# Turning the softmax weights, q and k of a layer on VectorE and GpSimd in place of TensorE and a round trip through DRAM

## The chip, the cores and the metric

The kernel runs on one core of one Trainium2 chip. A core has five engines that run side by side, each working through its own queue in order: TensorE (PE in the profile; its weight loads are PEld), VectorE (DVE), ScalarE (ACT), GpSimd (POOL) and SyncE (SP), which issues most DMAs. The metric is the device time of one execution in microseconds, as the median of several runs.

## What is computed

A two-layer encoder over 256 tokens of width 2048, batch 1, all in float32. Each layer has a mixer and a feed-forward part, both behind an RMS norm that is modulated by vectors made from a condition `c`. Cut to the part that the change touches:

```
h = rmsnorm(x) * (1 + scale) + shift
qa, ka, va, qb, kb, vb, ga, gb = split(h @ w_in)
qa, ka = rotary(rmsnorm(qa)), rotary(rmsnorm(ka))     # 8 query heads, 2 key heads of 128
qb, kb = rmsnorm(qb), rmsnorm(kb)                     # 8 heads of 128
ya = window_attention(qa, ka, va, sink) @ w_proj_a    # softmax(q k^T + mask) v, with a sink logit
yb = neighbourhood_attention(qb, kb, vb, bias) @ w_proj_b
x  = x + gate * ((sigmoid(ga) * ya + sigmoid(gb) * yb) @ w_out)
x  = x + gate2 * ((silu(conv(h2 @ w_up)_g) * conv(...)_v) @ w_down)
```

Two transposes hide in it. The projection gives q and k with tokens on the 128 partitions, and q k^T needs them with the head's 128 features there. The softmax gives its weights with queries on the partitions, and the product with v needs keys there.

## The kernel before

**The stream.** Each layer's weight matrices are cut into blocks of 128x128 in the order in which they are used, and 16 blocks make a unit of 1 MB, loaded by one DMA from SyncE's queue. A unit is used in two halves (`unit_steps`). Each float32 number is kept as a rounded high part and a remainder, so that three fast matmuls stand for one exact one: ScalarE casts a half to its high part (`hl`, L336) and VectorE subtracts to get the remainder (L337). Four half buffers turn round. TensorE consumes the stream in `features` (L355 to L357, output with features on the partitions, 256 columns) and in `tokens` (L418 to L420, tokens on the partitions, 512 columns); the nine column groups of q, k and v go through `tokens`, one group every four units.

**The background.** After each unit `Stream.tick` runs `bg.tick`: first what was put off to the next tick (`bg.defer`, `later`), then each background job by its pace, `ATT[l]` steps a tick for the attention while the q, k, v groups and the first gate pass, `ATT_B[l]` after the first projection. Other work is spread in between by plan, above all the modulation vectors: VectorE's multiply-and-reduce `aw` (L232). The order in which the instructions end up on each engine is made by a scheduler from the order of the program.

**q and k.** `qk_rows` takes a group's sums of squares on ScalarE (L588), a power -1/2 on GpSimd (`qrs`, L482), three ticks later the norm on VectorE (`qn`, L597) and, for the window heads, the rotary products and their sum and difference (L612 to L614). One tick later `turn` has TensorE transpose each head and half of the tokens into PSUM (`qtp`, L621), and ScalarE writes it with the gain into the group's `pack` (L622).

**A head.** `head_a` and `head_b` are generators that call `attend`; each `yield` is a step of the job, and in each step a new head starts and those under way advance. Scores on TensorE (`sc`, L648), maximum on VectorE (L651), exponential and division on ScalarE (L659, L667). Then, for heads that are not moved, four TensorE transposes (`tp`, L689); ScalarE and VectorE split the result into high part and remainder (`pT`, L430 and L431); a step later TensorE makes the output (`po`, L697). `MOVED[l]` gives how many window and neighbourhood heads of layer l are turned in another way: none but the eight neighbourhood heads of the second layer. For these VectorE transposes within blocks of 32x32 (L313), GpSimd's queue stores the rows block by block to DRAM (`pY`, L316, eight stores a head), and SyncE loads them back some ticks later (L299, two a head), the load held behind a subtraction of the stream (`BEHIND`).

Of the kernel before, what the change touches and what calls it, by code (L numbers as in the profile page):

```python
# [9 lines left out]
F32 = mybir.dt.float32  # L10
F32R = mybir.dt.float32r
AF = mybir.ActivationFunctionType
ALU = mybir.AluOpType
# [13 lines left out]
EPS = 1e-6  # L27
NEG = -1e30
SCALE = HEAD ** -0.5
BEHIND = mybir.DependencyInfo(mybir.DependencyClass.Sync, mybir.DependencyReason.DATA)  # L30
GRID_W, NA_KH, NA_KW = 64, 8, 16
BLOCK = 32

# [58 lines left out]
ADA_ORDER = [i for part in ADA_ORDER for i in part]  # L92
# [47 lines left out]
def encoder(ctx: ExitStack, tc: tile.TileContext, a: dict, out: bass.AP):  # L140
# [19 lines left out]
    dram = pool("dram", 2, space=bass.MemoryType.DRAM)  # L160

    ident = const.tile([P, P], F32, name="ident")
    make_identity(nc, ident[:])
# [43 lines left out]
    def paired(dt, name):  # L207

        t = ev.tile([P, 2 * S + ROW], dt, name=name, tag="u", bufs=2)
        return t[:, ROW - OFF : ROW - OFF + 2 * S].rearrange("p (a s) -> p a s", a=2)  # L210
# [71 lines left out]
                pass  # L282

    bg = Paced()
    halved = [None]

    def once(fn):

        due = [fn]

        def run():
            if due:
                due.pop()()

        return run

    def read_back(dst, src):

        tc.add_manual_dep(nc.sync.dma_start(dst, src).ins, halved[0], BEHIND)  # L299

    def later(n, fn):

        if n == 0:
            fn()
        else:
            bg.defer(lambda: later(n - 1, fn))

    def turned_blocks(p, rows, n, tag):

        y = dram.tile([P, n, S], F32, name=tag, tag=tag)  # L310
        to = y[:].rearrange("(b i) n (t a j) -> t a i n b j", i=BLOCK, t=2, a=P // BLOCK)
        for t, row in enumerate(rows):
            nc.vector.transpose(out=row, in_=p[t])  # L313
            src = row.rearrange("p (n b j) -> p n b j", n=n, j=BLOCK)
            for a in range(P // BLOCK):
                nc.gpsimd.dma_start(to[t, a], src[a * BLOCK : (a + 1) * BLOCK])  # L316
        return y

    def unit_steps(l, u, by_halves=False):

        raw = rawp.tile([P, UB * P], F32, name=f"w{l}_{u}", tag="raw")
        if not by_halves:
            nc.sync.dma_start(raw[:], a["ws"][l, u])
        halves = []
        streamed = any(m == "w_in" and mo < GATE_A // P for m, _, mo in STREAMS[l][u * UB : (u + 1) * UB])
        at = OFF if streamed else 0
        for j in range(2):
            n = UB * P // 2  # L330
# [5 lines left out]
            nc.scalar.copy(hl[:, 0], r)  # L336
            halved[0] = nc.vector.tensor_tensor(  # L337
                out=hl[:, 1], in0=r, in1=hl[:, 0].bitcast(F32), op=ALU.subtract
            ).ins.name
            halves.append(hl)  # L340
            if j == 0:
                yield halves
# [237 lines left out]
    def qk_rows(pss, heads, rot, gain, dst, then):  # L580
# [12 lines left out]
        rsqrt(rs[:, : 2 * heads], ss[:, : 2 * heads], HEAD, 2 * heads)  # L593
        def norm():
            qn = at.tile([P, 2, 4, HEAD], F32, name="qn", tag="qn", bufs=1)
            for t, ps in enumerate(pss):
                nc.vector.tensor_tensor(  # L597
                    out=qn[:, t, :heads],
                    in0=ps[:, cols : cols + n].rearrange("p (h d) -> p h d", d=HEAD),
                    in1=rs[:, t * heads : (t + 1) * heads].unsqueeze(2).broadcast_to([P, heads, HEAD]),  # L600
                    op=ALU.mult,
                )
            if rot is not None:
                x1, x2 = qn[:, :, :heads, :HALF], qn[:, :, :heads, HALF:ROT]
# [12 lines left out]
        def turn(qn):  # L617
            for t in range(2):
                ps = ax.tile([P, 4, P], F32, name="qtp", tag="ax")
                for h in range(heads):  # L620
                    nc.tensor.transpose(ps[:, h], qn[:, t, h], ident[:])  # L621
                nc.scalar.activation(  # L622
                    out=dst[:, :, t * P : (t + 1) * P], in_=ps[:, :heads], func=AF.Identity, scale=gain
                )
            then()

        bg.defer(lambda: bg.defer(lambda: bg.defer(norm)))
# [15 lines left out]
    def attend(q, k, v, p, mask, scale, sink, o, rows=None):  # L643
# [23 lines left out]
            nc.scalar.activation(out=p[:, t], in_=p[:, t], func=AF.Copy, scale=ri[:, t : t + 1])  # L667
        yield
        if rows is not None:
            rows = rows()  # L670
            y = turned_blocks([p[:, t] for t in range(2)], rows, 2, "pY")

            def back():
                for k in range(2):
                    read_back(rows[k], y[:, k])

            back = once(back)
            later(BACK[sink is None], back)
            yield
            yield  # L680
            back()
            pT = at.tile([P, 2, 2, S], F32R, name="pT", tag="pT", bufs=1)
            for k in range(2):
                split(pT[:, :, k], rows[k])
        else:
            tp = ax.tile([P, 2, S], F32, name="tp", tag="ax")
            for k in range(2):
                for t in range(2):
                    nc.tensor.transpose(tp[:, k, t * P : (t + 1) * P], p[:, t, k * P : (k + 1) * P], ident[:])  # L689
# [126 lines left out]
    for l in range(L):  # L816
# [41 lines left out]
        def head_a(i):  # L858
# [16 lines left out]
                return kvs[1]  # L875

            def rows():
                spare = ev.tile([P, S], F32, name=f"spare{l}_{i}", tag="r", bufs=2)
                return [qTa[:, i], spare[:]]
# [5 lines left out]
        def head_b(hb):  # L885
            b, i = packs[1 + hb // 4], hb % 4
            v = b[:, 4:8].rearrange("p (t a) s -> p t (a s)", t=2)
            p = at.tile([P, 2, S], F32, name="p", tag="p")
            nc.sync.dma_start(p[:], a["bias"][l, hb])
            q = in_halves(b[:, 8 + i], f"qB{l}_{hb}", "qh", l in SCORES_3)  # L890
            k = in_halves(b[:, i], f"kB{l}_{hb}", "kh", l in SCORES_3)
            yield
            yield from attend(
                q, k, lambda: in_halves(v[:, :, i * HEAD : (i + 1) * HEAD], f"vB{l}_{hb}", "vh", True), p, p, 1.0, None,
                lambda: oB_of(hb), (lambda: [b[:, 8 + i], b[:, i]]) if hb < MOVED[l][1] else None,
            )

        def oB_of(hb):
# [36 lines left out]
        for pi, (groups, gates) in enumerate(parts):  # L935
            last = pi == len(parts) - 1
            for g, part in enumerate(groups):
# [21 lines left out]
                    for t in range(2):  # L959
                        nc.scalar.copy(rows[:, t, vcol:], pss[t][:, vcol:])  # L960
                if g == 0:
                    qk_rows(pss, GA, rots[1], gains[:, 1:2], kTa, turned)
                elif g < 3:
                    qk_rows(pss, 4, rots[0], gains[:, 0:1], dst, turned)
                elif vcol is None:
                    qk_rows(pss, 4, None, gains[:, 3:4] if g in (3, 6) else gains[:, 2:3], dst, turned)
                else:
                    turned()
                if g == 2:
# [243 lines left out]
```

## Time and profile before

| | |
|---|---|
| Median of 3 runs | 2661.03 us (2660.66 to 2664.07) |
| Profiled execution, its own time | 2661.44 us |
| Its span in the trace | 2659.3 us |
| TensorE clock granted | full |
| Busy | PE 2647.6, PEld 2562.6, DVE 2106.2, ACT 1411.5, POOL 75.0 us |
| The second layer's q, k, v groups and heads | about 1400 to 1760 us |

Busy time is the time in which an engine had an instruction under way; an operation's row gives engine, line, output and inputs, shapes, count, then its busy time in us, the mean ns of one, and the idle time before it with what ended it. In a timeline the first two numbers are start and duration in us. The ends of matmuls are modelled, so matmuls are read by the distance of their starts. Times inside a part are from the start of the span.

### The profile page before, as it was taken

The numbers are of one execution on the slowest core, as the hardware profiler recorded it, in microseconds if no ns is written. First come the engines' busy times: TensorE is split into PE (matmuls) and PEld (weight loads), VectorE is DVE, ScalarE is ACT, GpSimd is POOL, SyncE is SP. The second block draws the span as 40 slices with busy tenths as digits, with TensorE's granted clock in tenths as the row PEclk, the third lists the DMA queues.
The fourth block names the chain that finished last, engine by engine and source line by source line (L and its number), as shares of the span: only waits on it lengthen the run. The fifth ranks groups of instructions, "written<-read, shape, count | busy, mean of one in ns | idle before, by whom it ended". The sixth has DMA issues, their size and how long they took to land.

```text
span 2659.3 us, 50973 instructions
## 1 busy us (share of the span) xinstructions
PE 2647.6 (100%) x21224; PEld 2562.6 (96%) x21224; DVE 2106.2 (79%) x2983; ACT 1411.5 (53%) x2292; POOL 75.0 (3%) x89
## 2 busy tenths in 40 slices
PE   9999999999999999999999999999999999999999
PEld 7888899999999999999998889999999999999999
DVE  8898998997987888788876666868888866655664
ACT  5445865456653554355554566555565445544553
POOL 0001100000000000000000001310000000000000
PEclk9999999999999999999999999999999999999999
DMA  9987789885777778788756666877747765555554
GB/s 365 349 327 297 264 300 351 321 311 212 290 295 286 296 290 287 288 297 296 295 205 256 236 229 238 299 264 261 278 179 287 297 251 191 191 197 194 196 191 143
DMA packets 106394, 704.63 MB, mean 265 GB/s; under 512 B 14001, under 2 KB 18353, under 8 KB 22321
## 3 DMA queue, kind: packets, MB, share of 16 engines
q1 hardware_dynamic: 104114, 699.27, 71.6%
q8 instruction: 166, 2.72, 0.4%
q0 software_dynamic: 2048, 2.10, 0.3%
q14 instruction: 66, 0.54, 0.1%
HBM read 697.13 MB, written 4.19 MB: 264 GB/s over the span
## 4 chain that ended last, share of the span: by engine, by line
PE 90%; DVE 5%; DMA 2%; ACT 1%; issue 1%; POOL 0%; DVEq 0%; ACTq 0%
PE ps L355 25%; PE ps L357 25%; PE ps L356 25%; PE ps_t L420 4%; PE ps_t L418 4%; PE ps_t L419 4%; DVE hl L337 2%; DVE aw L232 1%; DMA aw<-in_aw 1%; PE sc L648 1%; PE po L697 1%; ACT hl L336 1%; PE tp L689 0%; PE qtp L621 0%; DMA w<-in_ws 0%
## 5 line engine op out<-in xcount | busy, mean ns | idle before, releaser
L337 DVE TENSOR_TENSOR hl<-w,hl 128x1024 fp32r<-128x1024 f32 x928 | 1128.4, 1222 | 338.7 <-ACT hl L336 332.1
L336 ACT CAST hl<-w 128x1024 fp32r<-128x1024 f32 x928 | 970.6, 1049 | 738.3 <-PE ps L357 509.5
L355 PE MATMUL ps<-h,hl 128*128 128x256 f32 x3328 | 923.9, 278 | 1.3 <-DVE ya L979 0.6
L356 PE MATMUL ps<-h,hl 128*128 128x256 f32 x3328 | 921.1, 277 | 0.0
L357 PE MATMUL ps<-h,hl 128*128 128x256 f32 x3328 | 920.9, 277 | 0.0
L355 PEld LDWEIGHTS ps<-h,hl 128*128 128x128 f32 x3328 | 625.0, 188 | 2.4 <-DVE ya L979 0.8
L356 PEld LDWEIGHTS ps<-h,hl 128*128 128x128 f32 x3328 | 625.6, 188 | 0.4
L357 PEld LDWEIGHTS ps<-h,hl 128*128 128x128 f32 x3328 | 624.6, 188 | 0.0
L232 DVE CUSTOM_DVE_ANT_0 aw<-aw,cact,ab 128x2048 f32<-128x2048 f32 x189 | 443.5, 2347 | 61.1 <-DMA aw<-in_aw 60.4
L418 PE MATMUL ps_t<-hl,h 128*128 128x512 f32 x576 | 223.5, 393 | 2.1 <-ACT h L510 1.6
L419 PE MATMUL ps_t<-hl,h 128*128 128x512 f32 x576 | 225.1, 391 | 0.4
L420 PE MATMUL ps_t<-hl,h 128*128 128x512 f32 x576 | 224.6, 391 | 0.0
L1058 DVE SCALAR_TENSOR_TENSOR u<-ps,cw,u 128x255 f32<-128x255 f32 x304 | 146.2, 481 | 66.5 <-ACT u L1056 62.5
L1056 ACT ACTIVATE u<-ps,cw 128x256 f32<-128x256 f32 x152 | 85.7, 564 | 183.1 <-PE ps L357 183.0
L357 PE MATMUL ps<-merged,hl 128*128 128x256 f32 x512 | 141.8, 277 | 0.2 <-DVE hl L337 0.2
L355 PE MATMUL ps<-merged,hl 128*128 128x256 f32 x512 | 141.7, 277 | 0.0
L356 PE MATMUL ps<-merged,hl 128*128 128x256 f32 x512 | 141.7, 277 | 0.0
L356 PE MATMUL ps<-act_o,hl 128*128 128x256 f32 x512 | 141.6, 277 | 0.0
L357 PE MATMUL ps<-act_o,hl 128*128 128x256 f32 x512 | 141.6, 276 | 0.0
L355 PE MATMUL ps<-act_o,hl 128*128 128x256 f32 x512 | 141.4, 277 | 0.0
L418 PEld LDWEIGHTS ps_t<-hl,h 128*128 128x128 f32 x576 | 108.0, 188 | 25.5 <-ACT h L510 2.6
L419 PEld LDWEIGHTS ps_t<-hl,h 128*128 128x128 f32 x576 | 108.2, 188 | 24.0 <-DVE hl L337 2.1
(235 smaller groups left out, 4657.8 us busy)
## 6 DMA issues: line engine op xcount, KB each, us to landing
w<-in_ws SPq DMA_DIRECT2D x463, 1024.0 KB, 5.0
aw<-in_aw SPq DMA_DIRECT2D x189, 1024.0 KB, 6.1
p<-in_bias SPq DMA_DIRECT2D x16, 256.0 KB, 4.4
x<-in_xT SPq DMA_DIRECT2D x4, 512.0 KB, 5.5
aw_o<-in_aw SPq DMA_DIRECT2D x2, 1024.0 KB, 13.1
pY<-packB POOLq DMA_DIRECT2D x64, 32.0 KB, 4.2
packB<-pY SPq DMA_DIRECT2D x16, 128.0 KB, 2.7
out<-x SPq DMA_DIRECT2D x16, 128.0 KB, 2.6
```

Source lines behind the costliest of these rows:

```text
L232: nc.vector.tensor_tensor_reduce(out=raw[:], in0=raw[:], in1=cact[:], scale=1.0, scalar=ab[:, i : i + 1], op0=ALU.mult, op1=ALU.add, accum ...
L336: nc.scalar.copy(hl[:, 0], r)
L337: halved[0] = nc.vector.tensor_tensor(out=hl[:, 1], in0=r, in1=hl[:, 0].bitcast(F32), op=ALU.subtract).ins.name
L355: nc.tensor.matmul(out, hi, act[0], start=first, stop=False)
L356: nc.tensor.matmul(ps[:, :S], hi, act[1], start=False, stop=False)
L357: nc.tensor.matmul(out, lo, act[0], start=False, stop=last)
L418: nc.tensor.matmul(ps[:], xh, hi, start=kc == kcs[0], stop=False)
L419: nc.tensor.matmul(ps[:], xh, lo, start=False, stop=False)
L420: nc.tensor.matmul(ps[:], xl, hi, start=False, stop=kc == kcs[-1])
L648: nc.tensor.matmul(sc[:, t], q[i][:, t * P : (t + 1) * P], k[j], start=i + j == 0, stop=(i, j) == by(q)[-1])
L1056: nc.scalar.activation(out=u, in_=ps, func=AF.Identity, scale=w[:, 1:2], bias=w[:, 3:4])
L1058: nc.vector.scalar_tensor_tensor(out=u[:, to], in0=ps[:, of], scalar=w[:, j : j + 1], in1=u[:, to], op0=ALU.mult, op1=ALU.add)
```

## The change

In the second layer all sixteen heads' softmax weights (`MOVED` for that layer goes from (0, 8) to (8, 8)) and all seven groups of q and k are turned without TensorE and without DRAM. `turned_blocks` transposes within 32x32 blocks on VectorE into a spare buffer, and then GpSimd copies block columns between groups of 32 partitions back into the source, sixteen `tensor_copy` instructions on 32 partitions each. For a head a copy moves 128 elements a partition; for a group of four heads of q or k 256, and 128 for the first group, which has two. ScalarE then applies the gain from SBUF in one instruction over the group, one tick later (`QK_STEPS`); for a head the split follows one step later (`STEPS`). The first layer keeps its TensorE transposes. The store to DRAM, the loads back and what ordered them are removed. The attention's pace in the second layer goes from 0.4 to 0.43.

```diff
-ATT = [1.288, 0.4]
+ATT = [1.288, 0.43]
...
-BACK = [3, 4]
-MOVED = [(0, 0), (0, 8)]
+QK_STEPS = 1
+MOVED = [(0,0), (8,8)]
+STEPS = [1, 1]
...
-    def turned_blocks(p, rows, n, tag):
-
-        y = dram.tile([P, n, S], F32, name=tag, tag=tag)
-        to = y[:].rearrange("(b i) n (t a j) -> t a i n b j", i=BLOCK, t=2, a=P // BLOCK)
-        for t, row in enumerate(rows):
-            nc.vector.transpose(out=row, in_=p[t])
-            src = row.rearrange("p (n b j) -> p n b j", n=n, j=BLOCK)
-            for a in range(P // BLOCK):
-                nc.gpsimd.dma_start(to[t, a], src[a * BLOCK : (a + 1) * BLOCK])
-        return y
+    def turned_blocks(src, rows, n):
+
+        nc.vector.transpose(out=rows, in_=src)
+        blocks = rows.rearrange("p t (n k) -> p n t k", n=n)
+        dst = src.rearrange("p t (n k) -> p (t n k)", n=n).rearrange("p (n t k) -> p n t k", n=n, t=2)
+        for b in range(0, P, BLOCK):
+            for a in range(0, P, BLOCK):
+                nc.gpsimd.tensor_copy(
+                    out=dst[a : a + BLOCK, :, :, b : b + BLOCK], in_=blocks[b : b + BLOCK, :, :, a : a + BLOCK]
+                )
...
         def turn(qn):
+            if moved:
+                rows = dst.rearrange("p (t a) s -> p t (a s)", t=2)
+                src = qn.rearrange("p t h d -> p t (h d)")
+                turned_blocks(src, rows, heads)
+
+                def scaled():
+                    nc.scalar.activation(
+                        out=dst, in_=src.rearrange("p t (h d) -> p (t h d)", h=heads).rearrange("p (h s) -> p h s", h=heads),
+                        func=AF.Identity, scale=gain,
+                    )
+                    then()
+
+                later(QK_STEPS, scaled)
+                return
...
         if rows is not None:
-            rows = rows()
-            y = turned_blocks([p[:, t] for t in range(2)], rows, 2, "pY")
-
-            def back():
-                for k in range(2):
-                    read_back(rows[k], y[:, k])
-
-            back = once(back)
-            later(BACK[sink is None], back)
-            yield
-            yield
-            back()
-            pT = at.tile([P, 2, 2, S], F32R, name="pT", tag="pT", bufs=1)
-            for k in range(2):
-                split(pT[:, :, k], rows[k])
+            turned_blocks(p[:], rows(), 2)
+            for _ in range(STEPS[sink is None]):
+                yield
+            tp = p
         else:
...
-            pT = at.tile([P, 2, 2, S], F32R, name="pT", tag="pT", bufs=1)
-            split(pT, tp[:])
+        pT = at.tile([P, 2, 2, S], F32R, name="pT", tag="pT", bufs=1)
+        split(pT, tp[:])
```

The calls of `qk_rows` pass `l == 1` as `moved`, and the spare buffers are the group's own place in the `pack` for q and k, the places of heads already used for the window heads, and the head's own q and k for the neighbourhood heads.

More of the change, by code (lines that the diff above doesn't have):

```diff
@@ L284, in encoder @@
     bg = Paced()
[L285 to L299, printed above, removed]
     def later(n, fn):
@@ L336, in unit_steps @@
             nc.scalar.copy(hl[:, 0], r)
-            halved[0] = nc.vector.tensor_tensor(
-                out=hl[:, 1], in0=r, in1=hl[:, 0].bitcast(F32), op=ALU.subtract
-            ).ins.name
+            nc.vector.tensor_tensor(out=hl[:, 1], in0=r, in1=hl[:, 0].bitcast(F32), op=ALU.subtract)
             halves.append(hl)
@@ L578, in level, with qk_rows @@
             return z, sh
-    def qk_rows(pss, heads, rot, gain, dst, then):
+    def qk_rows(pss, heads, rot, gain, dst, then, moved=False):
         cols = 0
@@ L594, in norm @@
         def norm():
-            qn = at.tile([P, 2, 4, HEAD], F32, name="qn", tag="qn", bufs=1)
+            qn = at.tile([P, 8 * HEAD], F32, name="qn", tag="qn", bufs=1)[:, : 2 * n]
+            qn = qn.rearrange("p (t h d) -> p t h d", t=2, d=HEAD)
             for t, ps in enumerate(pss):
                 nc.vector.tensor_tensor(
-                    out=qn[:, t, :heads],
+                    out=qn[:, t],
                     in0=ps[:, cols : cols + n].rearrange("p (h d) -> p h d", d=HEAD),
@@ L603, in norm @@
             if rot is not None:
-                x1, x2 = qn[:, :, :heads, :HALF], qn[:, :, :heads, HALF:ROT]
+                x1, x2 = qn[:, :, :, :HALF], qn[:, :, :, HALF:ROT]
                 tab = [rot[:, i].unsqueeze(2).broadcast_to([P, 2, heads, HALF]) for i in range(4)]
@@ L877, in rows @@
             def rows():
-                spare = ev.tile([P, S], F32, name=f"spare{l}_{i}", tag="r", bufs=2)
-                return [qTa[:, i], spare[:]]
+                return qTa[:, i - 1 : i + 1] if i else paired(F32, f"spare{l}")
             yield from attend(
@@ L894, in head_b @@
                 q, k, lambda: in_halves(v[:, :, i * HEAD : (i + 1) * HEAD], f"vB{l}_{hb}", "vh", True), p, p, 1.0, None,
-                lambda: oB_of(hb), (lambda: [b[:, 8 + i], b[:, i]]) if hb < MOVED[l][1] else None,
+                lambda: oB_of(hb), (lambda: b[:, i : 9 + i : 8]) if hb < MOVED[l][1] else None,
             )
@@ L961, in encoder @@
                 if g == 0:
-                    qk_rows(pss, GA, rots[1], gains[:, 1:2], kTa, turned)
+                    qk_rows(pss, GA, rots[1], gains[:, 1:2], kTa, turned, l == 1)
                 elif g < 3:
-                    qk_rows(pss, 4, rots[0], gains[:, 0:1], dst, turned)
+                    qk_rows(pss, 4, rots[0], gains[:, 0:1], dst, turned, l == 1)
                 elif vcol is None:
-                    qk_rows(pss, 4, None, gains[:, 3:4] if g in (3, 6) else gains[:, 2:3], dst, turned)
+                    qk_rows(pss, 4, None, gains[:, 3:4] if g in (3, 6) else gains[:, 2:3], dst, turned, l == 1)
                 else:
```

2 lines of the change are left out of this document (removed).

## The prediction

> **What bounds the kernel now.** I read the page's busy shares first, then the chain that ended last, then the busy time by windows over the stretch in which the second layer's q, k and softmax weights are made.
>
> ```profile
> PE 2647.6 (100%) x21224; PEld 2562.6 (96%) x21224; DVE 2106.2 (79%) x2983; ACT 1411.5 (53%) x2292; POOL 75.0 (3%) x89
> PE 90%; DVE 5%; DMA 2%; ACT 1%; issue 1%; POOL 0%; DVEq 0%; ACTq 0%
> 1440.00:1640.00 200.00, 199.94 (x1086) 172.80 (x1085) 137.11 (x215) 123.24 (x273) 9.86 (x6) 1.00 0.63 234
> 1640.00:1760.00 120.00, 120.00 (x1053) 120.00 (x1053) 93.85 (x169) 70.02 (x132) 39.37 (x64) 1.00 0.80 279
> ```
>
> The last two lines are windows (us; then busy PE, PEld, DVE, ACT, POOL; clock; DMA share). The kernel is TensorE from end to end: 319.94 us busy in these 320 us, at full clock. So a matmul taken out shortens the run by what it takes, and nothing else does, as long as the next weights are ready. The question is therefore how far ahead they are.
>
> ```profile
> L337 DVE TENSOR_TENSOR hl<-w,hl 128x1024 fp32r<-128x1024 f32 x928 | 1128.4, 1222 | 338.7 <-ACT hl L336 332.1
> L336 ACT CAST hl<-w 128x1024 fp32r<-128x1024 f32 x928 | 970.6, 1049 | 738.3 <-PE ps L357 509.5
> 1470.60 1.05 ACT L336 CAST hl<-w 128x1024 fp32r<-128x1024 f32 x1 [1.67 <-PE ps_t L420]
> 1473.32 1.05 ACT L336 CAST hl<-w 128x1024 fp32r<-128x1024 f32 x1 [1.67 <-PE ps_t L420]
> ```
>
> A half unit of weights is cast by ScalarE (1.05 us), then VectorE subtracts (1.22). Casts come every 2.72 us, each set free by TensorE leaving a half, since there are four buffers. When a cast starts, three finished halves lie ahead of TensorE: 3 x 2.72 = 8.16 us. Cast and subtraction take 2.27, so a half may be 5.9 us late at no cost. Everything the change adds is paid for from these 5.9 us.
>
> **What it removes.** TensorE's 128x128 transposes of the second layer: 52 for q and k (one batch of 4, six of 8) and 32 for the eight window heads (eight of 4).
>
> ```profile
> 1461.07 0.39 PE L420 MATMUL ps_t<-hl,h 128*128 128x512 f32 x1
> 1461.30 1.03 PE L621 MATMUL qtp<-ident,qn 128*128 128x128 f32 x8
> 1462.09 0.48 PE L418 MATMUL ps_t<-hl,h 128*128 128x512 f32 x1
> 1462.41 0.39 PE L419 MATMUL ps_t<-hl,h 128*128 128x512 f32 x1
> ...
> 1438.77 0.39 PE L420 MATMUL ps_t<-hl,h 128*128 128x512 f32 x1
> 1439.01 0.60 PE L621 MATMUL qtp<-ident,qn 128*128 128x128 f32 x4
> 1439.36 0.51 PE L418 MATMUL ps_t<-hl,h 128*128 128x512 f32 x1
> 1439.70 0.40 PE L419 MATMUL ps_t<-hl,h 128*128 128x512 f32 x1
> ```
>
> By starts, a batch of 8 takes 0.79 and the matmul behind it 0.32 where such a one takes 0.23: 0.88 in all. A batch of 4 takes 0.35 + 0.11 = 0.46. So 6 x 0.88 + 0.46 + 8 x 0.46 = 9.4 us of TensorE go. The eight neighbourhood heads used no TensorE transposes before either; there the 64 stores from GpSimd's queue and SyncE's 16 loads go, which TensorE did not wait for (120.00 of 120.00 busy above), so I put that at nothing.
>
> **What it adds.** Per group of q or k (seven) and per head (sixteen): one block transpose on VectorE, sixteen GpSimd copies of 32 partitions, 368 in all, of 256 elements a partition for six groups and of 128 for the first group and the heads. ScalarE's gain operation now waits for the last copy of a group, its cast of the softmax weights for the last of a head. Both engines take their work in order, so a late copy holds the weight casts queued behind, and TensorE stops once 5.9 us are used up.
>
> ```profile
> L313 DVE STREAM_TRANSPOSE packB<-p 128x256 f32<-128x256 f32 x16 | 6.4, 430 | 1.7 <-ACT p L667 1.7
> L622 ACT ACTIVATE packB<-qtp,gains 128x512 f32<-128x512 f32 x16 | 10.5, 686 | 2.1 <-PE qtp L621 2.1
> L430 ACT CAST pT<-tp 128x512 fp32r<-128x512 f32 x24 | 14.1, 586 | 4.4 <-PE tp L689 4.4
> L232 DVE CUSTOM_DVE_ANT_0 aw<-aw,cact,ab 128x2048 f32<-128x2048 f32 x189 | 443.5, 2347 | 61.1 <-DMA aw<-in_aw 60.4
> 0.25 0.09 POOL L1205 MEMSET const-float32-0.0<- 128x1 f32 x1 [0.25 <-issue]
> 0.74 0.20 POOL masks.py:197 MEMSET ident<- 128x128 f32 x1 [0.29 <-POOLq L1205]
> 1.02 0.29 POOL masks.py:199 TENSOR_SCALAR_AFFINE_SELECT ident<-ident 128x128 f32<-128x128 f32 x1
> 1.29 0.71 POOL L172 TENSOR_TENSOR early<-early,mhalf 128x2 f32<-128x2 f32 x1
> L316 POOL DMA_DIRECT2D pY<-packB x64 | 39.4, 618 | 96.6 <-DVE packB L313 51.8 <-issue 44.4
> ```
>
> The block transpose of 256 elements takes 0.43, about what two-input VectorE operations of that size take; for 1024 I take the 1.22 of L337, for the gain operation on 1024 the 1.05 of L336 (two of 686 ns before). No GpSimd copy is in this trace. From below: the MEMSETs grow by 0.11 from 1 to 128 elements, so 0.11 for 128 and 0.22 for 256, if copies follow each other without a gap. From above: 0.62, GpSimd's dearest plain row, L316. Between them lies the one GpSimd row that reads and writes 128 elements a partition, the AFFINE_SELECT, with the next start 0.27 later. I take it: 0.27 for 128, 0.27 + 0.11 = 0.38 for 256. Sixteen copies are then 4.3 us for a head and 6.1 for a group.
>
> That would fit, were GpSimd alone. The trace shows that it is not: the same GpSimd power of 128x8 takes 1.64 us beside an idle VectorE, and more beside a busy one.
>
> ```profile
> 1467.79 1.64 POOL L482 TENSOR_TENSOR qrs<-qss,mhalf 128x8 f32<-128x8 f32 x1 [20.94 <-DVE qss L481]
> ...
> 247.25 2.35 DVE L232 CUSTOM_DVE_ANT_0 aw<-aw,cact,ab 128x2048 f32<-128x2048 f32 x1
> 247.38 3.72 POOL L482 TENSOR_TENSOR qrs<-qss,mhalf 128x8 f32<-128x8 f32 x1 [12.82 <-DVE qss L481]
> ...
> 259.13 4.08 POOL L482 TENSOR_TENSOR qrs<-qss,mhalf 128x8 f32<-128x8 f32 x1 [8.03 <-DVE qss L481]
> 259.36 2.36 DVE L337 TENSOR_TENSOR hl<-w,hl 128x1024 fp32r<-128x1024 f32 x2
> 261.63 1.29 DVE L949 TENSOR_TENSOR packB<-ps_t,packB 128x512 f32<-128x512 f32 x2
> ```
>
> 247.38 + 3.72 - 1.64 = 249.46 is the end of the L232 operation (249.60) within 0.15; 259.13 + 4.08 - 1.64 = 261.57 is where two L337 subtractions back to back end and L949 starts, which has one operand in PSUM. So GpSimd's reads wait while VectorE works on two SBUF operands, and need not get in between two such operations. [...]
>
> How full that port is, by L337, L232 and L431 in the same two windows (third number: VectorE us; L431 includes some PSUM reads):
>
> ```profile
> sum 320.00, DVE 128.67; mean DVE 64.33
> sum 320.00, DVE 42.37; mean DVE 21.19
> sum 320.00, DVE 23.16; mean DVE 11.58
> ```
>
> VectorE holds it some 194 of 320 us; 96 x 0.38 + 272 x 0.27 = 110 us of copies make 304. They fit on the mean; they do not where they must be done at a given time.
>
> **One group walked through**, the second of the window queries, in the order in which the changed program's instructions stand. Zero is the start of the cast whose subtraction precedes the transpose. That subtraction ends at 2.27, the rotary's two at 2.8, the transpose at 4.0. VectorE then has the next two subtractions (4.0 to 5.2; the second is cast only at 5.44 and runs 6.5 to 7.7) and an L232 (to 10.05). GpSimd gets 5.2 to 6.5, then all from 10.05, because VectorE's next subtraction needs a cast that stands behind the waiting gain operation. Copies done: 10.05 + 6.1 - 1.3 = 14.85. Gain 1.05, cast 1.05, subtraction 1.22: 18.2. TensorE wants that half at 3 x 2.72 + 8.16 = 16.3. It stops 1.9 us.
>
> The other groups the same way, each with the time until which VectorE's queue holds the port, and what GpSimd had by then: first keys (copies 4.3, gain 0.69 and a cast of 0.42) 8.9 and 0, late 0.3; first queries 7.7 and 1.8, late 0; first neighbourhood keys 8.6 and 0.3, late 1.4; then 13.4 and 2.6, late 3.9; 12.2 and 2.5, late 2.8. In the last group a head's sixteen copies stand in the middle of its own (10.4 us of work), 14.6 and 2.2: done 22.8, half ready 26.1, wanted 19.0, late 7.1. Sum 17.4 us.
>
> The heads cost nothing: their cast stands 4 to 9 halves (10.9 us or more) behind the transpose. The nearest, the first, has two: 7.7 + 4.3, then 0.59, 1.05, 1.22 make 14.9, under 16.3. VectorE's added transposes (7 groups, 8 window heads; the other eight had theirs) are in the walk or lie in its idle 63 us of the first window. The attention's pace of 0.43 for 0.4 and the changed number of steps leave the last output matmuls of both kinds ahead of the projections that read them; at nothing.
>
> **Sum.** 2661.4 us, the profiled execution's own time (span 2659.3), - 9.4 + 17.4 = 2669.4. The median of the three runs, 2661.0, is 0.4 lower: 2669.0. A measurement of this kernel tells 0.2%, 5.3 us, from no change: faster is below 2655.7, slower above 2666.4.
>
> **Rivals.** First, all copies stay hidden, and the run is faster. Place: GpSimd's sixteen copies between transpose and gain operation. If they read beside VectorE's subtractions, the walked group is done at 4.0 + 6.1 = 10.1 and its half at 13.4, ahead of 16.3; the others likewise: 2661.0 - 9.4 = 2651.6. With the port closed, the same needs copies near the lower bound: at 0.22 and 0.11 the three fullest groups are late 1.2, 0.1 and 1.8, giving 2654.7. It decides where a group's copies end within some 9 us of its transpose. For it: the powers of L482 read little and show nothing of a stream of reads; against it: their 4.08 us. [...]
>
> Second, the port changes hands between operations: GpSimd gets a copy in after each VectorE operation, and VectorE, delayed by 0.4 at a time, eats its own slack. About half of the lateness is left, 8 to 9 us, against 9.4 saved: 2660.5. The closed pair of L337 at 259.36 speaks against it.
>
> Third, copies are as dear as L316, 0.62: 9.9 us a set. Same walk: 5.4, 2.8, 5.7, 5.2, 7.7, 6.6 and 16.5 late, 50 us: 2701. Nothing but L316, whose work is of another kind, speaks for it.
>
> **Numbers.** Forecast, the port closed at the middle price, slower: 0.39, its own range 2663 to 2684 (0.06 of it within the band). First rival 0.33; second 0.20, of which 0.04 comes out faster and 0.03 slower; third 0.08. Slower 0.33 + 0.03 + 0.08 = 0.44, faster 0.33 + 0.04 - 0.02 (its worst end) = 0.35, same 0.21. The range for 8 in 10 reaches from the hidden case's 2651 to 2684 and leaves out the third rival and the tails.
>
> **What the changed profile would show.** Right: no L621 or L689 matmuls after 1400 us; 368 GpSimd copies with gaps or long spans whenever L337 or L232 runs; ScalarE idle before the gain operation, ended by GpSimd, most in the last group; TensorE idle 17 us between 1420 and 1640 before weights, ended by VectorE's L337. Wrong: TensorE still full there (first rival), copies of 256 elements spaced under 0.25 or over 0.5 us, L337 stretched or started late behind GpSimd (second), or idle TensorE before the heads' output matmuls, which I put at nothing.

## The result, and the profile after

| | before | after |
|---|---|---|
| Median | 2661.78 us of 4 runs (2660.66 to 2664.07) | 2705.15 us of 4 runs (2704.28 to 2708.15) |
| Profiled execution, its span | 2661.44, 2659.3 us | 2705.12, 2703.3 us |
| Ratio to before | | 1.0153, 95% interval 1.0137 to 1.0169 |

The change makes the kernel 43 us slower. The forecast was 2669.0 with a range from 2651 to 2684: the direction, to which it gave 0.44 against 0.35 for faster, was right, the size was not. One execution of the first kernel with the gain held back (below) took 4422.7 us at a granted clock of 0.557 and is left out of that kernel's median.

From the page of the kernel after: TensorE has 84 fewer instructions and yet more busy time.

```profile
PE 2655.5 (98%) x21140; PEld 2561.9 (95%) x21140; DVE 2125.2 (79%) x2982; ACT 1405.7 (52%) x2277; POOL 250.8 (9%) x393
```

The busy time by windows of both kernels over the stretch in which q, k and most heads are made (us; busy PE, PEld, DVE, ACT, POOL; clock; DMA share; GB/s), before and then after:

```profile
1400.00:1700.00 300.00, 299.94 (x1788) 265.88 (x1787) 209.20 (x335) 175.60 (x366) 30.65 (x39) 1.00 0.67 246
```

```profile
1400.00:1700.00 300.00, 265.97 (x1331) 223.54 (x1331) 190.64 (x280) 149.02 (x317) 159.27 (x265) 0.93 0.54 202
```

TensorE stands idle 34.0 us of these 300, where it was never idle before, and the granted clock falls to 0.93. The waits of the kernel after in that stretch (engine, line and what it waited for: us in total, times, longest) tell who is late for whom:

```profile
DVE hl L321 <- ACT hl L320: 61.2, 23, 11.2
ACT packB L607 <- POOL qn L299: 46.0, 4, 16.2
ACT packA L607 <- POOL qn L299: 30.1, 3, 11.8
PE ps_t L400 <- ACT hl L320: 19.5, 6, 8.6
PE ps L337 <- ACT hl L320: 8.1, 1, 8.1
PE ps_t L401 <- DVE hl L321: 5.9, 8, 1.7
```

Read from below: TensorE waits for the high part of weights from ScalarE (L320), then for short moments for the remainder from VectorE. ScalarE waits in seven gain operations (L607) for GpSimd's copies, 76.1 us together. VectorE then waits for ScalarE. Nobody is short of throughput: every engine but GpSimd is less busy here than before.

**One group.** The timeline of the kernel after around the second group, the first of the window queries, in order of start (start and duration in us; in brackets the idle time before it and what ended it):

```profile
1451.60 1.05 ACT L320 CAST hl<-w 128x1024 fp32r<-128x1024 f32 x1 [1.67 <-PE ps_t L402]
1453.69 1.29 DVE L580 TENSOR_TENSOR qn<-ps_t,qrs 128x512 f32<-128x512 f32 x2 [1.53 <-POOL qrs L464]
1457.04 1.05 ACT L320 CAST hl<-w 128x1024 fp32r<-128x1024 f32 x1 [1.67 <-PE ps_t L402]
1457.37 1.22 DVE L321 TENSOR_TENSOR hl<-w,hl 128x1024 fp32r<-128x1024 f32 x1
1458.51 1.24 DVE L294 STREAM_TRANSPOSE packA<-qn 128x1024 f32<-128x1024 f32 x1
1459.67 2.52 DVE L321 TENSOR_TENSOR hl<-w,hl 128x1024 fp32r<-128x1024 f32 x2
1459.81 8.77 POOL L299 COPY qn<-packA 32x256 f32<-32x256 f32 x16 [6.15 <-DVE packA L294]
1467.56 0.40 PE L402 MATMUL ps_t<-hl,h 128*128 128x512 f32 x1
1468.61 1.15 ACT L607 ACTIVATE packA<-qn,gains 128x1024 f32<-128x1024 f32 x1 [10.52 <-POOL qn L299]
1469.67 1.03 ACT L320 CAST hl<-w 128x1024 fp32r<-128x1024 f32 x1
1470.75 0.79 PE L400 MATMUL ps_t<-hl,h 128*128 128x512 f32 x1 [2.79 <-ACT hl L320]
1472.60 0.63 PE L402 MATMUL ps_t<-hl,h 128*128 128x512 f32 x1
1473.03 0.63 PE L400 MATMUL ps_t<-hl,h 128*128 128x512 f32 x1
```

ScalarE casts a half at 1457.04 and then sits 10.52 us in front of the gain. The next cast, which came 2.72 us after the one before so far, comes 12.63 later; TensorE has used up its three halves at 1467.96 and stops. When it goes on, its matmuls start 0.43 us apart instead of 0.23. A window before that stop, one behind it, and the other four stretches at the lower clock say why (us; busy PE, PEld, DVE, ACT, POOL; clock; DMA share; GB/s):

```profile
1460.00:1467.90 7.90, 7.90 (x35) 6.20 (x33) 2.19 (x2) 0.00 (x0) 7.32 (x15) 1.00 0.40 151
1470.60:1477.40 6.80, 6.19 (x14) 4.52 (x15) 6.26 (x8) 6.26 (x22) 0.27 (x1) 0.50 0.62 231
1497.90:1504.70 6.80, 6.25 (x14) 4.57 (x15) 4.78 (x5) 5.96 (x20) 0.83 (x1) 0.50 0.49 178
1576.40:1590.00 13.60, 5.67 (x13) 4.10 (x14) 5.70 (x7) 8.82 (x24) 6.51 (x14) 0.50 0.32 120
1614.00:1617.40 3.40, 2.94 (x7) 2.36 (x8) 3.40 (x6) 3.40 (x6) 2.27 (x2) 0.50 0.50 154
1672.00:1682.20 10.20, 5.79 (x25) 5.49 (x26) 5.14 (x10) 7.07 (x13) 1.63 (x6) 0.50 0.19 68
```

The clock was 1.00 and is 0.50. So a stop is paid twice, once while TensorE stands and once more while it runs slowly behind it. In the five windows TensorE is busy 26.8 us at 0.50, and half of that, 13.4 us, is lost to the clock.

**The sum of the 44.0 us** between the two spans: 34.0 us of idle TensorE, less 9.4 us of transposes that are gone; 2.6 us by which the profiled execution after was already late before anything changed, read from the cast of the same half unit, one row of each kernel:

```profile
1386.98 1.05 ACT L336 CAST hl<-w 128x1024 fp32r<-128x1024 f32 x1 [0.45 <-PE ps L357]
```

```profile
1389.60 1.05 ACT L320 CAST hl<-w 128x1024 fp32r<-128x1024 f32 x1 [0.45 <-PE ps L339]
```

The order of instructions up to there is the same in both; other kernels that share it are anything from 1.4 us early to 2.55 us late at this cast, so it is a matter of the execution. That leaves 44.0 - 34.0 + 9.4 - 2.6 = 16.8 us, of which the slow clock has 13.4. The remaining 3.4 is about what the stops cost beside their idle time, some 3.6 us by an estimate from the rows: before each of the 16 pieces of idle time the last matmul counts as busy for 0.28 to 0.79 us, where in the stream the next one would have started after 0.12 to 0.43.

### The profile page after: what moved, and what is told of

Its sections match the earlier page's. It is cut to its first block, busy times and chain, and to the rows that moved or that the text cites. A ratio compares the mean times of both kernels' runs of the same rounds, so it can differ in the third digit from the quotient of the medians.

```text
span 2703.3 us, 51016 instructions
## 1 busy us (share of the span) xinstructions
PE 2655.5 (98%) x21140; PEld 2561.9 (95%) x21140; DVE 2125.2 (79%) x2982; ACT 1405.7 (52%) x2277; POOL 250.8 (9%) x393
## 5 line engine op out<-in xcount | busy, mean ns | idle before, releaser
L321 DVE TENSOR_TENSOR hl<-w,hl 128x1024 fp32r<-128x1024 f32 x928 | 1130.1, 1225 | 329.4 <-ACT hl L320 327.3
L320 ACT CAST hl<-w 128x1024 fp32r<-128x1024 f32 x928 | 967.9, 1048 | 689.0 <-PE ps L339 472.7
L337 PE MATMUL ps<-h,hl 128*128 128x256 f32 x3328 | 923.7, 278 | 9.4 <-ACT hl L320 8.3
L337 PEld LDWEIGHTS ps<-h,hl 128*128 128x128 f32 x3328 | 626.0, 188 | 10.6 <-ACT hl L320 8.9
L231 DVE CUSTOM_DVE_ANT_0 aw<-aw,cact,ab 128x2048 f32<-128x2048 f32 x189 | 444.4, 2352 | 75.3 <-DMA aw<-in_aw 74.6
L400 PE MATMUL ps_t<-hl,h 128*128 128x512 f32 x576 | 227.6, 400 | 22.0 <-ACT hl L320 20.0
L401 PE MATMUL ps_t<-hl,h 128*128 128x512 f32 x576 | 229.9, 400 | 6.3 <-DVE hl L321 5.9
L402 PE MATMUL ps_t<-hl,h 128*128 128x512 f32 x576 | 227.7, 396 | 0.0
L337 PE MATMUL ps<-merged,hl 128*128 128x256 f32 x512 | 142.0, 278 | 1.7 <-DVE m L426 1.7
L337 PE MATMUL ps<-act_o,hl 128*128 128x256 f32 x512 | 141.2, 276 | 0.0
```

The lines of the kernel that those rows point to most:

```text
L231: nc.vector.tensor_tensor_reduce(out=raw[:], in0=raw[:], in1=cact[:], scale=1.0, scalar=ab[:, i : i + 1], op0=ALU.mult, op1=ALU.add, accum ...
L321: nc.vector.tensor_tensor(out=hl[:, 1], in0=r, in1=hl[:, 0].bitcast(F32), op=ALU.subtract)
L337: nc.tensor.matmul(out, hi, act[0], start=first, stop=False)
L400: nc.tensor.matmul(ps[:], xh, hi, start=kc == kcs[0], stop=False)
L401: nc.tensor.matmul(ps[:], xh, lo, start=False, stop=False)
L402: nc.tensor.matmul(ps[:], xl, hi, start=False, stop=kc == kcs[-1])
```

## The experiments

My theory was that the place of the wait decides: the gain stands in ScalarE's in-order queue ahead of the weight casts, and the copies are done too late for it. The rival was that the copies as such, 368 of them beside VectorE's own work, cost the time wherever the waiting instruction stands.

**Only the heads.** `qk_rows` in the second layer gets no `moved`, so q and k stay on TensorE.

```diff
-                    qk_rows(pss, 4, rots[0], gains[:, 0:1], dst, turned, l == 1)
+                    qk_rows(pss, 4, rots[0], gains[:, 0:1], dst, turned)
```

(and the same in the other two calls)

> Only the sixteen heads' softmax weights are turned by blocks and copies; q and k go through TensorE as in the kernel before. Theory (a late turn holds ScalarE's queue: its gain operation waits for the last of a group's sixteen copies, weight casts queue behind it, TensorE runs dry for 34 us and then runs 17 us slower at a lower granted clock): the seven gain operations no longer wait for GpSimd, TensorE keeps its 52 q/k transposes and loses only the 32 of the window heads, 8 x 0.46 = 3.7 us; the heads' own split stands late enough: 2661.7 - 3.7 = 2658, at most 2665 if the one wait of 7.4 us at a head's split stays. Rival (GpSimd's copies slow the stage as such, wherever the consumer stands): 256 of the 368 copies stay, so about two thirds of the 52 us lost: 2690.

Measured: 2659.08 against 2660.83 us before, ratio 0.9992 (0.9983 to 1.0001), not told from no change. In more rounds, once beside four groups of q and k and once beside three (below):

> The heads alone once more, in five rounds beside the run before, to tell 3.7 us from nothing. Theory: 2661 - 3.7 = 2657 to 2658. Rival: no gain, 2661.

Measured: 2657.84 against 2661.43, ratio 0.9984 (0.9975 to 0.9993).

> The heads alone, beside the run before on the same chip: 2657 to 2658 by both theories; what the three groups add is read against it.

Measured: 2659.49 against 2664.77, ratio 0.9982 (0.9972 to 0.9992). TensorE's window in the last of the three:

```profile
1400.00:1700.00 300.00, 299.80 (x1788) 265.94 (x1788) 224.70 (x351) 178.37 (x373) 137.21 (x215) 1.00 0.65 240
```

256 of the 368 copies are in this kernel, and so are the pace of 0.43 and the missing round trip through DRAM; GpSimd is busy 137 us, and TensorE is full at full clock. The three comparisons gave 1.8, 3.6 and 5.3 us, and the window heads' transposes are 8 x 0.46 = 3.7 us. The rival had 2690: the heads' copies do not cost by their presence. This version beats both kernels, the one before by 0.08 to 0.18%, of which the first comparison alone could be nothing.

**Only q and k.** The heads go through TensorE, all sixteen.

```diff
-MOVED = [(0,0), (8,8)]
+MOVED = [(0,0), (0,0)]
```

> Only q and k are turned by blocks and copies; all sixteen heads' softmax weights go through TensorE. Theory: the gain operations still wait; the two longest waits (16.2 and 14.4 us), which had a head's copies ahead of or among the group's on GpSimd, shrink by 12 x 0.33 = 4 and 5.2 us, so idle falls from 34 to 24 us and the slow clock behind it from 17 to 12: 2661.7 - 5.7 (q/k transposes gone) + 3.7 (eight neighbourhood heads now transposed on TensorE) + 36 = 2696. Rival (the copies as such): 112 of 368 copies stay, a third of the 52 us: 2661.7 - 2 + 16 = 2676.

Measured: 2693.69 against 2660.83, ratio 1.0122 (1.0106 to 1.0137); 2 us from the theory, 18 from the rival. The waits at the gains, with their longest:

```profile
ACT packA L607 <- POOL qn L299: 31.5, 3, 13.0
ACT packB L607 <- POOL qn L299: 30.2, 4, 9.9
```

61.7 us instead of 76.1, and the 16.2 us are gone. That was the wait of the fifth of the seven groups, and its reason is in the kernel after: its copies stood behind a head's on GpSimd.

```profile
1565.35 1.25 DVE L294 STREAM_TRANSPOSE packB<-qn 128x1024 f32<-128x1024 f32 x1
1564.91 6.30 POOL L299 COPY p<-packA 32x128 f32<-32x128 f32 x12
1571.27 9.17 POOL L299 COPY qn<-packB 32x256 f32<-32x256 f32 x16
```

The group is turned at 1566.60; its first copy starts 4.7 us later.

**The gain a step later.**

```diff
-QK_STEPS = 1
+QK_STEPS = 2
```

> The changed kernel with the gain operation issued two steps of the weight stream (four half units) behind the transpose instead of one; all copies stay. Theory: ScalarE reaches the gain operation 2 x 2.72 = 5.4 us later, so the waits that stopped TensorE by 3.3, 4.7, 1.3 and 4.1 us go, those of 10.3 and 8.5 leave 4.9 and 3.1, with about 4 us at the lower clock behind them: 2661.7 - 9.4 + 8 + 4 = 2664. Rival (the copies as such): nothing changes, 2700 to 2705.

Measured: 2709.34 against 2660.83, ratio 1.0178 (1.0163 to 1.0193). By the numbers this is the rival's result, and it would have refuted the theory had the edit done what it says. It did not: in ScalarE's order all seven gains stand behind the same weight casts as before the edit, so the scheduler's order did not follow the step count. The gains waited about as long as ever, 71.4 us together where it had been 76.1. So this run decides nothing between the two; the three further down repeat it with the place held.

**The gain on GpSimd.**

```diff
-                def scaled():
-                    nc.scalar.activation(
-                        out=dst, in_=...
-                        func=AF.Identity, scale=gain,
-                    )
-                    then()
-
-                later(QK_STEPS, scaled)
+                nc.gpsimd.tensor_scalar(
+                    out=dst, in0=...
+                    scalar1=gain, scalar2=None, op0=ALU.mult,
+                )
+                later(QK_STEPS, then)
```

> The changed kernel with the gain multiplied by GpSimd right behind its sixteen copies (one operation of 128x1024, about 1.0 us by the copies' 0.29 at 128 and 0.39 at 256 elements) instead of by ScalarE; all copies stay, and GpSimd works 7 us more. Theory: ScalarE has nothing left to wait for until the heads' splits, so the seven waits go and TensorE stays full but for those splits: 2652 to 2660. Rival (the copies as such): GpSimd is busier than before, 2705 or more.

Measured: 2686.5 against 2660.83, ratio 1.0099 (1.008 to 1.0117): 19 us better than the kernel after, though GpSimd works more, but far from the 2652 to 2660 expected. Three things went otherwise. The multiplication took 2.85 us and not 1.0 (the operation's rows: durations ns minimum, median, maximum). ScalarE only waits further on, at the splits of the first heads' k and q and, 21.4 us in five waits, at the splits of softmax weights. And VectorE's norm waits for GpSimd's power, which stands behind copies and multiplications in GpSimd's queue; the longest of these waits, 12.5 us, ended at 1588.25, and TensorE's longest stop, 8.5 us, ended with the subtraction behind it:

```profile
L606 POOL TENSOR_SCALAR packB<-qn,gains x4: 2853/2856/6014, 1521.8 to 1672.0; 128x1024 f32<-128x1024 f32 x4
```

```profile
DVE qn L580 <- POOL qrs L464: 26.4, 7, 12.5
ACT qA L412 <- POOL packA L606: 13.1, 1, 13.1
ACT kA L412 <- POOL packA L606: 9.5, 1, 9.5
```

**VectorE's large two-operand operations out of the way.** The `aw` operations (L231) between the 8th and the 50th unit are packed behind.

```diff
-ADA_PLAN_1 = [(8, 143), (76, 166), ...
+ADA_PLAN_1 = [(8, 143), (50, 143), (76, 166), ...
```

> The changed kernel with the modulation's multiply-and-reduce operations (L231, 2.35 us, two SBUF operands) planned out of the stretch: none between the 8th and 50th unit of the second layer, the 23 that stood between there and the 76th unit packed into the last 26 units. Nothing else is changed. Theory (a group's sixteen copies take 6.3 us by themselves and are shut out while VectorE works on two SBUF operands): five of the seven groups had one L231 within their copies; their waits fall by 2.35 us each and TensorE's idle by about 9 of 34 us, the slow clock behind it by some 3: 2693. Rival (the copies are simply too many, VectorE's operands do not matter): 2705, unchanged. Packing the operations later may itself cost something there, which would show as idle TensorE after the groups.

Measured: 2685.9 against 2661.98, ratio 1.0094 (1.0079 to 1.0109). TensorE's idle in the 300 us falls from 34.0 to 17.3 and the clock rises to 0.98:

```profile
1400.00:1700.00 300.00, 282.66 (x1556) 243.84 (x1556) 188.07 (x294) 162.62 (x343) 162.78 (x293) 0.98 0.50 184
```

No copy, gain or wait was touched, and the third group's sixteen copies take 8.79 us where the kernel after had 10.72 (its row is further down):

```profile
1476.34 8.79 POOL L299 COPY qn<-packA 32x256 f32<-32x256 f32 x16 [6.15 <-DVE packA L294]
```

So the time of GpSimd's copies does depend on what VectorE runs beside them. Not all of the gain is theirs, though: with fewer operations in its queue VectorE also finished three of the seven transposes earlier, the last one 6.0 us after the cast of the half subtracted before it, where it had been 9.6, and this run does not tell the two apart. The gain was larger than expected (19 us for 12): idle time in the stretch fell by 16.7 us and not by 9, of which 4.8 came back behind 1700 us, and the slow clock cost 5.1 us (10.2 us busy at 0.50), 8.3 less than before and not 3. Stops of 0.3 to 1.7 us after 1700 us show where the operations went.

**The gain held further back.** ScalarE's cast is noted, and the gain is ordered behind the newest one; both run on ScalarE, and the order costs no wait of its own: in the waits of the three kernels the gains wait for GpSimd alone, 55.2, 27.7 and 12.3 us. `QK_STEPS` is 1, 2 and 3 in three kernels.

```diff
-            nc.scalar.copy(hl[:, 0], r)
+            halved[0] = nc.scalar.copy(hl[:, 0], r).ins.name
...
-                    nc.scalar.activation(
+                    gained = nc.scalar.activation(
...
+                    tc.add_manual_dep(gained.ins, halved[0], BEHIND)
```

> The run before this one that issued the gain two steps later did not move it: the scheduler put it back between the same weight casts. Here the gain is tied behind the newest weight cast on ScalarE, so that the seven gains stand 3, 1, 2, 3, 2, 3 and 2 half units (2.72 us each) further back in ScalarE's order; the copies and everything else stay. Theory: TensorE's seven stops of 0.8, 3.3, 4.7, 1.3, 10.3, 4.1 and 8.5 us shrink to 0, 0.6, 0, 0, 4.9, 0 and 3.1, with about 5 us at the lower clock behind the last: 2661.7 - 9.4 + 8.6 + 5 = 2666. Rival (the copies as such): 2700 to 2709, as with the step count alone.

Measured: ratio 1.0121 (1.0104 to 1.0138), 2692.8 us.

> As the run before, with the gain 5, 3, 4, 5, 4, 5 and 4 half units (8.2 to 13.6 us) further back than in the changed kernel. Theory: every stop of the seven goes; what is left are ScalarE's splits of the heads: 2661.7 - 9.4 = 2652, at most 2657. Rival (the copies as such): 2700 to 2709.

Measured: ratio 1.0082 (1.0067 to 1.0097), 2683.5 us.

> As the run before, with the gain 7, 5, 6, 7, 6, 7 and 6 half units further back. Theory: the same 2652 to 2657, unless q and k now come too late for the heads, whose scores would then wait. Rival (the copies as such): 2700 to 2709.

Measured: ratio 1.0049 (1.0033 to 1.0066), 2674.2 us, against 2661.98 before for all three.

With every copy in place, 31 of the 43 us go by moving seven instructions back in ScalarE's queue: 2705, 2693, 2684, 2674. In the third the gains wait 12.3 us for copies where it had been 76.1. So much is the place of the wait. But each step gave less than the theory's 2666 and 2652, and the rows say where at least a part of the rest went. In the third, a set of copies takes longer than the same set did in the kernel after:

```profile
1450.87 14.62 POOL L301 COPY qn<-packA 32x256 f32<-32x256 f32 x16 [5.79 <-DVE packA L296]
```

14.62 us instead of 8.77 for the same group, because VectorE is no longer starved by ScalarE: it works some 9.8 us on two SBUF operands in that time (six L323 and one L232), and the copies take 7.7 more than 16 x 0.397 and 15 pauses of 0.04 between them. In the 8.77 us of the kernel after it had worked 2.4, until 1462.19, and then waited for ScalarE. And VectorE has a wait of its own now, here in the second of the three:

```profile
1602.55 0.71 DVE L296 STREAM_TRANSPOSE packA<-p 128x512 f32<-128x512 f32 x1 [7.19 <-POOL p L301]
1605.42 3.76 DVE L323 TENSOR_TENSOR hl<-w,hl 128x1024 fp32r<-128x1024 f32 x3
```

The next head's block transpose writes the buffer that the last head's copies still read; three subtractions of weights stand behind it, and TensorE stopped 5.4 us there. So the rival is right in part: with most of the wait out of the way some 22 us above the theory's 2652 are left, and what these rows show is copies that hold GpSimd, and with it VectorE. How the 22 us divide I have not separated.

**The first groups only.** Heads and four groups, then heads and three, the gains held back by three steps; the other groups on TensorE.

```diff
-                    qk_rows(pss, 4, None, ..., dst, turned, l == 1)
+                    qk_rows(pss, 4, None, ..., dst, turned, l == 1 and g == 3)
```

(the second of the two has no `moved` there at all)

> All sixteen heads' softmax weights and the first four groups of q and k (the window keys, both of the window queries, the first of the neighbourhood keys) are turned by blocks and copies, the gain tied 5 to 7 half units further back as in the run before; the last three groups, whose copies shared GpSimd with the heads', go through TensorE again. Theory: the first four groups caused no stop any more when the gain stood so far back, and the heads alone caused none, so nothing stops: 8 x 0.46 for the heads, 0.46 and 3 x 0.88 for the groups make 6.8 us saved: 2655. Rival (the copies as such): 320 of 368 copies stay, 2670 or more.

Measured: 2659.68 against 2661.43, ratio 0.9992 (0.9983 to 1.0001).

> All sixteen heads and the first three groups (the window keys and both of the window queries) are turned by blocks and copies, the gain tied 5 to 7 half units further back; all four neighbourhood groups go through TensorE. In the run with four groups the first three gained 2.2 us by the times of the weight casts, and stops of 0.4 to 0.8 us came only after the fourth group, whose copies ran until just before the first head's. Theory: without the fourth, 8 x 0.46 + 0.46 + 2 x 0.88 = 5.9 us saved and no stop: 2655 to 2656. Rival (each group moved costs something wherever its gain stands): 2660 as with four groups.

Measured: 2662.93 against 2664.77, ratio 0.9988 (0.9978 to 0.9999).

Neither gains more than the heads alone, beside which both ran. By the times of the weight casts the first three groups do bring 2.2 us, as counted, in both. What takes them back: k comes later, so ScalarE's split of the first head stands seven half units further back than in the kernel with the heads alone, the later heads crowd, and stops of 0.2 to 0.8 us, 2.8 us together in the kernel with four groups, come back between 1540 and 1690. That the crowding makes these stops is argued from the order and not tested; I have not tried to place the heads by hand.

## Why the prediction failed, step by step

- **TensorE's 9.4 us.** Right as far as it could be seen alone: 1.8, 3.6 and 5.3 us measured for the heads' 3.7, and 2.2 by the casts for the first three groups' 0.46 + 2 x 0.88.
- **The price of a copy.** Right for one copy, too low for sixteen. The answer for the copies' line in the kernel after, durations in ns minimum, median and maximum:

```profile
L299 POOL COPY p<-packB x128: 284/293/2413, 1682.2 to 1794.2; 32x128 f32<-32x128 f32 x128
L299 POOL COPY qn<-packB x64: 390/397/2492, 1509.2 to 1673.4; 32x256 f32<-32x256 f32 x64
```

  0.29 and 0.40 us against 0.27 and 0.38 forecast. But the forecast's were distances from start to start, and between two copies lie another 0.04 us: 0.33 and 0.44. A head's sixteen take 5.2 us with nothing in the way and not 4.3, a group's would take 7.0 and not 6.1, so up to 0.9 us were missing from each stop. The lower bound that I had worked out from the MEMSETs, 0.22 us for 256 elements, holds only for the slope: 128 more elements cost 0.107 us, and by that slope some 0.18 us of the 0.29 (my estimate) come on top of every copy.
- **The closed port.** Right while one VectorE operation runs, wrong between two. ("Port" is my word; what the runs show is copies that last until a VectorE operation on two SBUF operands is over.) The longest copies, 2.4 us, are as long as an L231, 2.35. But where one VectorE operation follows the next at once, a waiting copy gets in between, here in the fourth group of the kernel after:

```profile
1509.04 1.18 DVE L321 TENSOR_TENSOR hl<-w,hl 128x1024 fp32r<-128x1024 f32 x1
1509.18 1.30 POOL L299 COPY qn<-packB 32x256 f32<-32x256 f32 x1 [3.67 <-DVE packB L294]
1510.14 2.48 DVE L231 CUSTOM_DVE_ANT_0 aw<-aw,cact,ab 128x2048 f32<-128x2048 f32 x1
1510.51 2.37 POOL L299 COPY qn<-packB 32x256 f32<-32x256 f32 x1
1512.55 1.41 DVE L321 TENSOR_TENSOR hl<-w,hl 128x1024 fp32r<-128x1024 f32 x1
```

  Each copy ends 0.26 us behind the VectorE operation that it waited for, and the operation that follows is longer for it, 2.48 us where 2.35 is the mean and 1.41 where 1.22 is. The subtractions of the same stretch, L321 after and L337 before, in ns minimum, median and maximum:

```profile
L321 DVE TENSOR_TENSOR hl<-w,hl x87: 1180/1225/1420, 1399.4 to 1698.6; 128x1024 fp32r<-128x1024 f32 x87
L337 DVE TENSOR_TENSOR hl<-w,hl x101: 1214/1225/1227, 1399.4 to 1697.9; 128x1024 fp32r<-128x1024 f32 x101
```

  So GpSimd did get a copy in between operations, as in the second rival, but this cost VectorE 0.1 to 0.2 us at a time and not 0.4, and the lateness did not halve as that rival had it. The walk gave the second of the window queries 14.85 - 4.0 = 10.85 us from transpose to last copy, and its sixteen took 10.72:

```profile
1484.91 10.72 POOL L299 COPY qn<-packA 32x256 f32<-32x256 f32 x16 [6.14 <-DVE packA L294]
```

  That it fits so well is luck: five copies were through just behind VectorE's last operation there, where the walk had the time of 3.4, and the other eleven followed 0.44 us apart and not 0.38.
- **When the group is turned.** Wrong, the first failed step. The walk, of the third group, let VectorE finish the transpose 4.0 us behind its zero. Measured, group by group: 5.2, 8.1, 7.7, 5.0, 6.8, 8.6 and 9.6. VectorE was already behind: in the rows of one group above, the norm waits for GpSimd's power until 1453.69, and the subtraction at 1457.37 is, by count, that of the half cast at 1451.60, 5.8 us earlier. The walk had 1.05 us there. Of the difference 1.6 us could have been read in the trace before, where the subtraction of the same half starts at 1450.56 and its cast at 1447.90; the rest came up in the kernel after, where VectorE had just waited 2.92 us, until 1448.60, for the load of an `aw`. So a part of the 5.9 us of slack was spent before this group's copies began. The other half of the walk was right: TensorE wanted its half at 16.3 and stopped at 1467.96, 16.36 after the cast of 1451.60.
- **A head's copies in a group's way.** I counted that for the last group alone. It held the fifth of the seven too, by 4.7 us.
- **The seven stops.** Forecast 0.3, 0, 1.9, 1.4, 3.9, 2.8 and 7.1, together 17.4 us. Measured, in the same order: 0.9, 3.3, 4.7, 1.3, 10.3, 4.1 and 8.5, with small ones between 34.0 in all. The long ones end with ScalarE's cast, not with VectorE's subtraction as forecast, because a half's first matmul needs the high part alone; the moments after it, 0.5 to 1.7 us, in which TensorE waits for the remainder, are counted in.
- **The clock behind a stop.** Missing from the sum: 13.4 us, and some 3.4 that a stop costs beside its idle time. With the 16.6 us by which the idle time was forecast too short, this is the failed step that made the size wrong. Nothing in the trace before could price it, since TensorE was busy 319.94 of the 320 us there, and I set it to nothing without a word.
- **The heads.** Right that they cost nothing by themselves.

So 2669.0 + 16.6 for longer stops + 13.4 for the clock + 3.4 beside them + 2.6 of the execution give 2705.0, measured 2705.15; it closes because the 3.4 is what was left. The rival with copies as dear as L316 had 2701 (the first of its seven terms is 5.9 by the walk's own numbers and not 5.4, which changes little), close to the result for a reason that the rows refute. The rival in which everything stays hidden is true of the heads alone.

## What to carry to other kernels

Before moving work to a side engine, look for the instruction that waits for its last result and count what stands behind that one in its queue: here sets of sixteen copies on GpSimd cost nothing that could be measured where their consumer stood far back and only the heads' sets were there, and seven of them cost 43 us where it stood two half units behind them. A step count in the program does not move an instruction if a scheduler orders it; read the order, and pin it. Price a stop of TensorE at more than its idle time (here another 16.8 us on 34.0, of which 13.4 for the clock), and do not read a side engine's time from a stretch in which the others are starved.

## What I had not expected of the hardware

- TensorE's granted clock fell to 0.50 after stops that are short. In the first of the kernels with the gain held back, a stop of 1.64 us, one matmul, and 0.76 us more were enough:

```profile
1464.76 0.39 PE L404 MATMUL ps_t<-hl,h 128*128 128x512 f32 x1
1466.79 0.50 PE L402 MATMUL ps_t<-hl,h 128*128 128x512 f32 x1 [1.64 <-ACT hl L322]
1468.05 0.52 PE L403 MATMUL ps_t<-hl,h 128*128 128x512 f32 x1 [0.76 <-DVE hl L323]
1471.36 0.60 PE L402 MATMUL ps_t<-hl,h 128*128 128x512 f32 x1
1471.78 0.41 PE L403 MATMUL ps_t<-hl,h 128*128 128x512 f32 x1
```

  The starts are 0.41 to 0.43 us apart from 1468.39 until 1471.78, where they had been 0.23 before the stop; the clock was 1.00 from 1460.0 to 1468.0, 0.56 from there to 1471.0 and 0.90 over the next 4 us. In the kernel after, 0.53 and 0.77 us, with one matmul between them, were not enough at 1522: the clock stayed at 1.00 until 1530. What decides it these runs do not show. Five of the stops of the kernel after cost 1.5 to 3.1 us each in this way.
- While VectorE worked on two SBUF operands, GpSimd's copies stood still for most of it: 7.7 us of 9.8 in the set of 14.62. In the rows of the fourth group one copy got through at each of two changes from one operation to the next, and the next one was 0.1 to 0.2 us longer for it.
- GpSimd's multiplication by a per-partition scalar took 2.85 us for 1024 elements and 1.57 for 512 in the kernel with the gain there, where copies in the kernel after took 0.107 us per 128 more elements.
